# A hybrid attention block: c4 ahead of q's chunk, four staging buffers, V turned at the end of the head, branch products ahead of the weighted sum

## The chip, the cores and the metric

The kernel runs on one core of one Trainium2 chip. The core has five engines with instruction streams of their own: TensorE (PE, with its weight loads listed as PEld), VectorE (DVE), ScalarE (ACT), GpSimd (POOL) and SyncE (SP). They meet through semaphores; an engine carries out its own stream strictly in order, so an instruction that waits also holds up whatever stands behind it. The metric is the device time of one execution in microseconds, and lower is better.

## The reference, cut to what matters

One layer over 512 tokens of width 1024, with 16 learned meta tokens in front (528 in all). All of it is fp32.

```python
xn = rmsnorm(h)
sb_q, sb_k, sb_v, df_q, df_k, df_v = split(xn @ w_in)      # 8 heads of 128 in each branch
# branch A, stick-breaking: z = q.k / sqrt(128), strictly causal
u = where(causal, log_sigmoid(-z), 0); rest = reverse_cumsum(u) - u
o_sb = where(causal, exp(log_sigmoid(z) + rest), 0) @ v
# branch B, differential: two softmax maps of 64 channels each, with bias and chunk mask
o_df = rmsnorm_per_head((softmax(s0) - lam * softmax(s1)) @ v)
merged = sigmoid(gate0) * (o_sb @ w_br_sb) + sigmoid(gate1) * (o_df @ w_br_df)
h = h + merged @ w_out
h = h + (silu(hn @ w_ffn_gate) * (hn @ w_ffn_up)) @ w_ffn_down   # hn = rmsnorm(h)
return rmsnorm(h)
```

## The kernel before

**Numbers in two pieces.** Every fp32 factor of a large product is held as a high piece (a cast, made by ACT) and a low piece (the rest, made by DVE); one product is three matmuls, hi x hi, lo x hi and hi x lo, at lines 227, 228 and 229. A weight chunk is split into `wh` at line 75 (ACT) and `wl` at line 76 (DVE).

**The order of the work.** After an opening (to about 40 us), eight stick-breaking heads run one after another, then eight differential heads, then gates and merge, the output projection, the feed-forward layer and its down projection. A head's attention is a generator (`sb_head`, `df_head`). While it runs, the projections of the next head and pieces of the branch product of an earlier pair of heads are interleaved as "units": each `yield n` of the generator lets n units through, and what is left over runs at the head's end. A scheduler then places the instructions of each engine in a fixed order by its own estimates, near the order in which the program issues them.

**Seven products.** From head `SEVEN` on, k and v of a head are projected together with seven half-size products in place of eight. The units `u1` to `u4` need sums of weight blocks: `c1` splits v's chunk g; `c2` forms the sum s out of k's chunk u, which is staged as `wsu`, and g (lines 173 and 174, on DVE), and splits it; `c3` adds g and u inside `wsu` (line 181) and splits that; `c4` adds into g's second half (line 188) and splits the half. q's chunk is split plainly (`generic`). The list `prep` gives the order in which chunks are prepared: here, for each such head, c1, c2, c3, then q's chunk, then c4, and a chunk of the branch product's weights behind them. A unit that needs an entry first has the list prepared up to `READY` entries further.

**Staging.** SP's queue brings chunks from DRAM in the order of the list `stream`, 512 KB each, into `wst` (three buffers here) or, for a k chunk of such a head, into `wsu` (one buffer in the attention's pool, so that the next k chunk's transfer can only be issued once the split of c3, `wl<-wsu`, has read this one).

**A head's end.** The units `t1` and `t2` (`turn_first`, `turn_rest`) turn the attention weights (lines 493, 507, 510), with the pieces a_h and a_l at lines 495 and 496. `av` (`weighted`) is the weighted sum over V. In a stick-breaking head its result is taken out of a bank of the score tile (two such tiles of two banks, in turn) at lines 590 (o_h) and 591 (o_l); the next head's scores use the same tiles, zA for the first three query blocks and zB for the fourth. `turn` turns V of the next head (vT to vh, vl, vf; lines 469 to 477); here it is one of the units, between the first and the second unit of the branch product. A unit of the branch product (`y_units`) forms two blocks of 128 x 512, copies each out on ACT, and has POOL's queue store it (the first two products of a branch) or add it into DRAM, 256 KB a block; a head carries four blocks.

In a differential head the scores go through `biased` (line 636, two maps of each query block), `maps` makes the softmax, and the evacuations of q (lines 604 and 605) and k (611 and 612) hold copies for both maps; two DMAs of POOL's queue bring halves of dk to the other partitions (line 615).

## Time and profile before

| what | value |
|---|---|
| three runs | 1001.55, 998.5, 1000.55 us; median 1000.55 |
| profiled execution | 998.36 us, its span 996.6 us |
| granted TensorE clock | 0.995 |
| PE / DVE / ACT / POOL busy | 96% / 71% / 60% / 16% |
| stick-breaking heads with seven products (from 108 us) | 28.00 us each, PE busy throughout |
| differential heads (from 248 us) | 31 to 32 us each, PE busy 27.53 to 29.73 us |
| 517 to 632 us (gates, merge, output projection) | PE busy 114.99 of 115 us |
| 665 to 980 us (feed-forward) | PE busy 314.56 of 315 us |

The tensor engine is the busy one; where it is busy throughout, work on the other engines costs nothing unless it makes PE wait. In a timeline the columns are start, duration, engine, line, operation, out<-in, and in brackets the engine's idle time before the instruction with what ended it. `wl<-wsu` and the like name the tiles without buffer numbers.

### The profile page before, as it was taken

To read this page: it belongs to the slowest core of one execution; us is meant where nothing else is said; L and a number is where in the kernel's file an instruction comes from. 1 tells how busy PE (TensorE), PEld (TensorE's weight loads), DVE (VectorE), ACT (ScalarE), POOL (GpSimd) and SP (SyncE) were. 2 spreads that over 40 slices of the span, in tenths; PEclk is the share of its full clock that TensorE was granted. 3 is DMA by queue.
4 is the path that set the end of the run, shared out by engine and by line. 5 is a ranking of instruction groups with operands and counts; after the bars stand their busy time and mean duration, and the time that the engine had idled before them with its cause. 6 is when DMAs were issued, how large, how long until landed. Compare 5 with 4: busy or idle time off the path is not lost.

```text
span 996.6 us, 16149 instructions
## 1 busy us (share of the span) xinstructions
PE 958.2 (96%) x6117; PEld 857.3 (86%) x6117; DVE 711.1 (71%) x1284; ACT 600.8 (60%) x1147; POOL 160.5 (16%) x216
## 2 busy tenths in 40 slices
PE   7999999999989999999999999989999999999996
PEld 4998888889877898778878888879999999988885
DVE  8898687777767977788642633799888888754544
ACT  5666666667577877778772533675555555743533
POOL 4010111111232222323313520000000000000103
PEclk9999999999999999999999999999999999999999
DMA  7212434445654444547838732223333333333212
GB/s 214 86 43 65 127 113 105 109 105 127 148 100 115 97 137 129 105 108 207 174 91 199 228 117 86 84 84 107 103 110 100 113 95 118 102 110 100 92 43 85
DMA packets 140240, 114.12 MB, mean 115 GB/s; under 512 B 4961, under 2 KB 115714, under 8 KB 140162
## 3 DMA queue, kind: packets, MB, share of 16 engines
q1 hardware_dynamic: 129810, 89.29, 29.7%
q0 software_dynamic: 10192, 23.73, 12.4%
q8 instruction: 48, 0.79, 0.3%
q14 instruction: 30, 0.25, 0.1%
q10 hardware_dynamic: 160, 0.07, 0.0%
HBM read 89.87 MB, written 18.87 MB: 109 GB/s over the span
## 4 chain that ended last, share of the span: by engine, by line
PE 66%; DVE 17%; ACT 7%; DMA 5%; issue 4%; POOL 0%; SPq 0%; ACTq 0%; DVEq 0%; POOLq 0%
PE mm L227 15%; PE mm L229 15%; PE mm L228 15%; PE z L227 6%; PE z L229 6%; PE z L228 6%; DMA wsu<-in_w_in_dram 4%; DVE wl L76 3%; DVE pr L636 2%; ACT wh L75 1%; ACT pr L660 1%; DVE dq L605 1%; PE z L493 1%; DVE dk L612 1%; DVE s L578 1%
## 5 line engine op out<-in xcount | busy, mean ns | idle before, releaser
L76 DVE TENSOR_TENSOR wl<-wst,wh 128x1024 fp32r<-128x1024 f32 (+1 forms) x150 | 166.4, 1114 | 90.5 <-ACT wh L75 90.5
L75 ACT CAST wh<-wst 128x1024 fp32r<-128x1024 f32 (+1 forms) x150 | 142.1, 948 | 87.9 <-PE z L229 37.8
L227 PE MATMUL mm<-xT_h,wh 128*128 128x512 f32 (+2 forms) x496 | 168.7, 340 | 0.1
L228 PE MATMUL mm<-xT_l,wh 128*128 128x512 f32 (+2 forms) x496 | 168.4, 340 | 0.4 <-DVE xT_l L828 0.2
L229 PE MATMUL mm<-xT_h,wl 128*128 128x512 f32 (+2 forms) x496 | 167.4, 338 | 0.0
L227 PEld LDWEIGHTS mm<-xT_h,wh 128*128 128x128 f32 x496 | 93.9, 189 | 10.3 <-ACT xT_h L827 1.0
L228 PEld LDWEIGHTS mm<-xT_l,wh 128*128 128x128 f32 x496 | 93.6, 189 | 10.2 <-DVE xT_l L828 0.6
L229 PEld LDWEIGHTS mm<-xT_h,wl 128*128 128x128 f32 x496 | 93.6, 189 | 9.8
L228 PE MATMUL mm<-hT_l,wh 128*128 128x256 f32 x284 | 80.6, 284 | 0.7 <-DVE hT_l L1074 0.7
L227 PE MATMUL mm<-hT_h,wh 128*128 128x256 f32 x284 | 80.5, 285 | 0.6 <-DVE sg L1169 0.6
L229 PE MATMUL mm<-hT_h,wl 128*128 128x256 f32 x284 | 80.2, 283 | 0.0
L227 PE MATMUL mm<-o_h,wh 128*128 128x512 f32 x128 | 53.5, 420 | 9.2 <-DVE dq L605 8.8
L228 PEld LDWEIGHTS mm<-hT_l,wh 128*128 128x128 f32 x284 | 53.8, 189 | 1.1 <-DVE hT_l L1074 1.1
L227 PEld LDWEIGHTS mm<-hT_h,wh 128*128 128x128 f32 x284 | 53.5, 189 | 1.0 <-DVE sg L1169 0.8
L173 DVE TENSOR_TENSOR s<-wsu 128x512 f32<-128x512 f32 x35 | 27.4, 783 | 37.2 <-DMA wsu<-in_w_in_dram 28.4
L229 PEld LDWEIGHTS mm<-hT_h,wl 128*128 128x128 f32 x284 | 53.7, 189 | 0.0
L229 PE MATMUL mm<-o_h,wl 128*128 128x512 f32 x128 | 50.6, 397 | 0.0
L228 PE MATMUL mm<-o_l,wh 128*128 128x512 f32 x128 | 50.3, 394 | 0.0
L76 DVE TENSOR_TENSOR wl<-wsu,wh 128x1024 fp32r<-128x1024 f32 x35 | 42.8, 1223 | 8.9 <-ACT wh L75 8.7
L227 PE MATMUL mm<-t_h,wh 128*128 128x256 f32 x168 | 47.5, 283 | 1.3 <-ACT wh L75 1.0
L475 POOL COPY v_s<-vT 128x16 f32<-128x16 f32 x64 | 22.3, 497 | 163.8 <-DVE vT L405 78.1
L228 PE MATMUL mm<-t_l,wh 128*128 128x256 f32 x168 | 47.2, 281 | 1.1 <-DVE t_l L1089 1.1
(316 smaller groups left out, 2776.4 us busy)
## 6 DMA issues: line engine op xcount, KB each, us to landing
wst<-in_w_in_dram SPq DMA_DIRECT2D x32, 512.0 KB, 4.4
wst<-in_w_ffn_gate_dram SPq DMA_DIRECT2D x22, 512.0 KB, 3.9
wst<-in_w_ffn_down_dram SPq DMA_DIRECT2D x22, 512.0 KB, 3.6
wsu<-in_w_ffn_up_dram SPq DMA_DIRECT2D x21, 512.0 KB, 3.7
wst<-in_w_gate_dram SPq DMA_DIRECT2D x16, 512.0 KB, 4.6
wsu<-in_w_in_dram SPq DMA_DIRECT2D x14, 512.0 KB, 6.5
y_df<-ys POOLq DMA_DIRECT2D x20, 256.0 KB, 5.9
dk<-dk POOLq DMA_DIRECT2D x16, 264.0 KB, 3.6
```

The source lines that it names most:

```text
L75: (hi_copy or nc.scalar.copy)(hi, src)
L76: (lo_eng or nc.vector).tensor_tensor(lo, src, hi.bitcast(F32), op=ALU.subtract)
L173: nc.vector.tensor_tensor(s[:, K2], u[:, K1], u[:, K2], op=ALU.add)
L227: nc.tensor.matmul(ps, lhsT=ah, rhs=bh, start=(start and i == 0), stop=False, skip_group_check=skip)
L228: nc.tensor.matmul(ps, lhsT=ah, rhs=bl, start=False, stop=False, skip_group_check=skip)
L229: nc.tensor.matmul(ps, lhsT=al, rhs=bh, start=False, stop=(stop and i == n - 1), skip_group_check=skip)
L475: nc.gpsimd.tensor_copy(v_s[:, 32 * t:32 * t + NM], vT[:, (t + 1) * P:(t + 1) * P + NM])
L493: nc.tensor.transpose(pt[:, (t - j) * P:(t - j + 1) * P], blocks(t, j * P, (j + 1) * P), ident)
L578: nc.vector.tensor_tensor_scan(f, f, f, 0.0, op0=ALU.add, op1=ALU.bypass)
L605: nc.vector.scalar_tensor_tensor(q[c][b], ps[a], DF_SCALE, q[c][a].bitcast(F32), op0=ALU.mult, op1=ALU.subtract)
L612: nc.vector.scalar_tensor_tensor(k[c][a, 1, s], ps[a], scale, k[c][a, 0, s].bitcast(F32), op0=ALU.mult, op1=ALU.subtract)
L636: nc.vector.tensor_tensor_reduce(po, zz, bb, scale=1.0, scalar=-3.0e38, op0=ALU.add, op1=ALU.max, accum_out=mx[:, t, c:c + 1])
```

## The change

It does four things. Four buffers, not three, for the staged chunks. In `prep`, c4 stands directly behind c3, ahead of the same head's q chunk. `turn` is no longer a unit: it runs at the end of the loop's body, behind the weighted sum and all units, and so vf, vh and vl have one buffer each. And the yields let more units through ahead of the weighted sum. To make room, `y_back` uses the tags of o_h and o_l, and the feed-forward's `sq` has a tag of its own with one buffer.

```diff
--- before.py
+++ after.py
@@ -138,7 +138,7 @@
         elif sevens(key) and key[2] == 1:
             st = fpools["a"].tile([P, KT, P], F32, tag="wsu", name="wsu")
         else:
-            st = wpool.tile([P, k1 - k0, cw], F32, tag="wst", bufs=3, name="wst")
+            st = wpool.tile([P, k1 - k0, cw], F32, tag="wst", bufs=4, name="wst")
         staged.append(st)
         for a, b in ((0, 4), (4, 8)) if n < 2 else ((0, k1 - k0),):
             nc.sync.dma_start(st[:, a:b], view[:, k0 + a:k0 + b, c0:c0 + cw])
@@ -195,7 +195,7 @@
         key = stream[n][0]
         fns = [] if sevens(key) else [generic]
         if sevens(key) and key[2] < 2:
-            fns = [c1, c2, c3] if key[2] else [generic, c4]
+            fns = [c1, c2, c3, c4] if key[2] else [generic]
         for fn in fns:
             prep_at[key if fn is generic else (fn, key[0:2])] = len(prep)
             prep.append((fn, n if fn is generic else key[0:2]))
@@ -461,9 +461,9 @@
 
         def turn():
 
-            vf = ap_.tile([P, 2, P], F32, tag="vf", bufs=2, name="vf")
-            vh = ap_.tile([P, 3, P], F32R, tag="vh", bufs=2, name="vh")
-            vl = ap_.tile([P, 3, P], F32R, tag="vl", bufs=2, name="vl")
+            vf = ap_.tile([P, 2, P], F32, tag="vf", name="vf")
+            vh = ap_.tile([P, 3, P], F32R, tag="vh", name="vh")
+            vl = ap_.tile([P, 3, P], F32R, tag="vl", name="vl")
             pt, p5 = tr_tile(), tr_tile()
             for j in range(4):
                 nc.tensor.transpose(pt[:, j * P:(j + 1) * P], vT[:, j * P:(j + 1) * P], ident)
@@ -585,7 +585,7 @@
         t1()
         yield 1
         t2()
-        yield 1
+        yield 2
         ps = av()
         nc.scalar.copy(o_h, ps)
         nc.vector.tensor_tensor(o_l, ps, o_h.bitcast(F32), op=ALU.subtract)
@@ -679,9 +679,8 @@
         t1, t2, av = attn_out(lambda t, k0, k1: prs[t][:, 0, k0:k1], d, 64)
         yield 3 if h < NH - 1 else 2
         t1()
-        yield 1
         t2()
-        yield 1
+        yield 2
         ps = av()
         of = ap_.tile([P, SEQ], F32, tag="of", name="of")
         sq = ap_.tile([P, SEQ], F32, tag="sq", name="sq")
@@ -941,7 +940,7 @@
                 sg0 = [gate_tile(br) for br in range(2)]
                 units = more + gate(0, 0, sg0[0], AF.Identity) + gate(1, 0, sg0[1], AF.Identity)
             else:
-                units = units + more[0:1] + [turn] + more[1:]
+                units = units + more
             if (br, h) == (0, 0):
                 for i, u in enumerate(sums):
                     units[i] = lambda a=units[i], b=u: (a(), b())
@@ -950,6 +949,8 @@
                     units.pop(0)()
             for u in units:
                 u()
+            if turn:
+                turn()
             d = nd
             if h % 2:
                 todo += [y_units(name, h - 1 + i, o) for i in range(2)]
@@ -973,8 +974,8 @@
 
     def y_back(f):
         got = []
-        for name in ("y_sb", "y_df"):
-            y = mgp.tile([P, SEQ], F32, tag=name, name=name, bufs=2)
+        for name, tag in (("y_sb", "o_h"), ("y_df", "o_l")):
+            y = opool.tile([P, 2, SEQ], F32, tag=tag, name=name)[:, 0]
             nc.sync.dma_start(y, y_part[name][f])
             got.append(y)
         return got
@@ -1029,7 +1030,7 @@
                     step(k, t, c0, c1)
                 cs = slice(half * 512 + c0, half * 512 + c1)
                 nc.vector.tensor_tensor(hres[:, t, cs], hres[:, t, cs], (acc[t] if c0 == 0 else extra)[:, c0:c1], op=ALU.add)
-                sq = pool.tile([P, 512], F32, tag="y_sb", bufs=2, name="sq")
+                sq = pool.tile([P, 512], F32, tag="sq", bufs=1, name="sq")
                 s0, s1 = ssq[t][:, 0:1], ssq[t][:, 1:2]
                 nc.scalar.activation(sq[:, c0:c1], hres[:, t, cs], AF.Square, accum_out=(s1 if half else s0))
                 if half == 0:
```

The same instructions are issued; they stand in another order. On DVE, in a stick-breaking head, between the split of c3 and the next head's scores, before (s_2005 and s_2316 are the sums of two heads; L591 is o_l, L472 V's low piece):

```order
L76 TENSOR_TENSOR wl<-wsu,wh 128x1024
L514 COPY a_s<-z 16x32 x2
L188 TENSOR_TENSOR wst<-s_2005,wst 128x512
L591 TENSOR_TENSOR o_l<-z,o_h 128x512
L472 TENSOR_TENSOR vl<-tr,vh 128x384
L173 TENSOR_TENSOR s_2316<-wsu 128x512
L76 TENSOR_TENSOR wl<-wst,wh 128x1024
```

and with the change:

```order
L76 TENSOR_TENSOR wl<-wsu,wh 128x1024
L514 COPY a_s<-z 16x32 x2
L188 TENSOR_TENSOR wst<-s_2005,wst 128x512
L76 TENSOR_TENSOR wl<-wst,wh 128x512
L173 TENSOR_TENSOR s_2316<-wsu 128x512
L174 TENSOR_TENSOR s_2316<-s_2316,wst 128x512
L591 TENSOR_TENSOR o_l<-z,o_h 128x512
L472 TENSOR_TENSOR vl<-tr,vh 128x384
```

c4's split (128x512) has moved up ahead of the next head's sum, and the two halves of that sum, L173 and L174, have moved ahead of o_l and V's piece.

Further on in the same head on DVE, around the scans (L578; the split `wl<-wst,wh 128x1024` is q's chunk), before:

```order
L173 TENSOR_TENSOR s_2316<-wsu 128x512
L76 TENSOR_TENSOR wl<-wst,wh 128x1024
L384 TENSOR_TENSOR vT<-mm,qq 128x264
L574 SCALAR_TENSOR_TENSOR s<-z,e 128x832
L574 SCALAR_TENSOR_TENSOR s<-z,e 128x528
L578 SCALAR_TENSOR_TENSOR s<-s 128x144
L578 SCALAR_TENSOR_TENSOR s<-s 128x272
L578 SCALAR_TENSOR_TENSOR s<-s 128x416
L578 SCALAR_TENSOR_TENSOR s<-s 128x528
L579 TENSOR_TENSOR s<-z,s 128x832
L579 TENSOR_TENSOR s<-z,s 128x528
L396 SCALAR_TENSOR_TENSOR qq<-mm,qq 128x264
```

and with the change:

```order
L574 SCALAR_TENSOR_TENSOR s<-z,e 128x832
L384 TENSOR_TENSOR vT<-mm,qq 128x264
L578 SCALAR_TENSOR_TENSOR s<-s 128x144
L578 SCALAR_TENSOR_TENSOR s<-s 128x272
L578 SCALAR_TENSOR_TENSOR s<-s 128x416
L574 SCALAR_TENSOR_TENSOR s<-z,e 128x528
L579 TENSOR_TENSOR s<-z,s 128x832
L578 SCALAR_TENSOR_TENSOR s<-s 128x528
L76 TENSOR_TENSOR wl<-wst,wh 128x1024
L396 SCALAR_TENSOR_TENSOR qq<-mm,qq 128x264
L579 TENSOR_TENSOR s<-z,s 128x528
```

q's split stood second, ahead of the whole chain; now it stands behind the last scan.

On DVE in a differential head, between the split of c3 and the first biased scores (L636), before (L496 is a_l, L514 the small transposed blocks):

```order
L76 TENSOR_TENSOR wl<-wsu,wh 128x1024
L496 TENSOR_TENSOR a_l<-z,a_h 128x384
L496 TENSOR_TENSOR a_l<-z,a_h 128x256
L472 TENSOR_TENSOR vl<-tr,vh 128x384
L188 TENSOR_TENSOR wst<-s_4775,wst 128x512
L514 COPY a_s<-z 16x64 x2
L173 TENSOR_TENSOR s_5145<-wsu 128x512
L636 ISA pr,mx<-z,bias 128x144
```

and with the change:

```order
L76 TENSOR_TENSOR wl<-wsu,wh 128x1024
L496 TENSOR_TENSOR a_l<-z,a_h 128x384
L514 COPY a_s<-z 16x64 x2
L188 TENSOR_TENSOR wst<-s_4790,wst 128x512
L76 TENSOR_TENSOR wl<-wst,wh 128x512
L173 TENSOR_TENSOR s_5160<-wsu 128x512
L174 TENSOR_TENSOR s_5160<-s_5160,wst 128x512
L472 TENSOR_TENSOR vl<-tr,vh 128x384
L636 ISA pr,mx<-z,bias 128x144
```

L173 stood ahead of L636 already; L174, V's piece and c4's split now stand there too, and V's piece behind L173.

## The prediction

> **What bounds the kernel now.** I read the page first, then the busy times by stretch of one head each, the waits, and the timelines of one head of each branch.
>
> ```profile
> PE 958.2 (96%) x6117; PEld 857.3 (86%) x6117; DVE 711.1 (71%) x1284; ACT 600.8 (60%) x1147; POOL 160.5 (16%) x216
> PE 66%; DVE 17%; ACT 7%; DMA 5%; issue 4%; POOL 0%; SPq 0%; ACTq 0%; DVEq 0%; POOLq 0%
> L173 DVE TENSOR_TENSOR s<-wsu 128x512 f32<-128x512 f32 x35 | 27.4, 783 | 37.2 <-DMA wsu<-in_w_in_dram 28.4
> ...
> 164.00:192.00 28.00, 28.00 (x185) 24.99 (x183) 20.55 (x33) 18.59 (x34) 5.04 (x8) 1.00 0.52 113
> 279.00:310.00 31.00, 27.53 (x177) 24.51 (x176) 24.64 (x61) 22.88 (x54) 9.62 (x13) 1.00 0.54 119
> 342.00:373.00 31.00, 28.72 (x184) 25.54 (x183) 24.16 (x61) 22.85 (x54) 8.13 (x13) 1.00 0.41 119
> 517.00:632.00 115.00, 114.99 (x510) 95.13 (x511) 47.15 (x58) 43.42 (x67) 33.90 (x24) 1.00 0.54 151
> ```
>
> In the stretches the columns are the length, then PE, PEld, DVE, ACT, POOL. A stick-breaking head is all PE (28.00 of 28): nothing can be gained there, and each new PE wait is paid in full. A differential head leaves PE idle 2.3 to 3.5 us of 31: that is all there is to gain. Gates, merge and output projection (517 to 632) are full; y's new staging tags and sq's single buffer change nothing on PE there, so I cost them at 0; in the opening, one c2 sum moves up, also 0 (at worst one such sum, 0.8). All the rest is the two kinds of head.
>
> The idle time of the differential heads has two owners:
>
> ```profile
> PE mm L227 <- DVE dq L605: 8.8, 6, 2.5
> PE z L227 <- DVE a_l L496: 6.1, 6, 1.0
> ```
>
> Columns: total us, times, longest. Six heads, so 1.5 and 1.0 us a head: a projection product waits for the bank that q's evacuation frees, and the weighted sum waits for DVE's piece of the weights.
>
> **The change in the stick-breaking heads.** With c4 ahead of q's chunk, DVE meets L173, which waits for the staged chunk wsu, ahead of the evacuation o_l (L591), and o_l holds a score bank that the next head's last scores need. Before, o_l stood ahead:
>
> ```profile
> 166.62 1.22 DVE L76 TENSOR_TENSOR wl<-wsu,wh 128x1024 fp32r<-128x1024 f32 x1
> 168.73 0.69 DVE L188 TENSOR_TENSOR wst<-s,wst 128x512 f32<-128x512 f32 x1
> 170.81 0.69 DVE L591 TENSOR_TENSOR o_l<-z,o_h 128x512 fp32r<-128x512 f32 x1 [1.39 <-ACT o_h L590]
> 171.42 0.55 DVE L472 TENSOR_TENSOR vl<-tr,vh 128x384 fp32r<-128x384 f32 x1
> 173.13 0.69 DVE L173 TENSOR_TENSOR s<-wsu 128x512 f32<-128x512 f32 x1 [1.17 <-DMA wsu<-in_w_in_dram]
> ...
> 167.92 0.37 SPq L144 DMA_DIRECT2D wsu<-in_w_in_dram  x1
> ...
> 163.95 0.86 PE L493 MATMUL z<-ident,s 128*128 128x128 f32 x5
> 174.86 0.37 PE L227 MATMUL z<-kh,qh 128*128 128x264 f32 x1
> ```
>
> The single wsu buffer is still released by `wl<-wsu` alone. Count from E = 163.95, the end of u4. PE does the same matmuls between u4 and those scores (B = 174.86), so it arrives at E + 10.9 as before. Two more a_l pieces stand ahead of `wl<-wsu` than before; I put its end at E + 4.65 (it was E + 3.9, 0.75 less) and the DMA 0.06 behind. With D from issue to L173's start, o_l ends at E + 4.7 + D + 0.62 (L173) + 0.62 (L174) + 0.69 (o_l): the scores wait S = D - 4.2 (rounded, with 0.06 for the signal). V's turn, vl, stands behind o_l and costs nothing there. What was D?
>
> ```profile
> 140.41 0.38 SPq L144 DMA_DIRECT2D wsu<-in_w_in_dram  x1
> 144.50 0.69 DVE L173 TENSOR_TENSOR s<-wsu 128x512 f32<-128x512 f32 x1 [0.38 <-DMA wsu<-in_w_in_dram]
> ...
> GB/s 0 0 0 0 0 155 93 0 0 0 185 124 185 201 216 170 216 247 147 205 309 325 352 348 305 301 301 294 301 282 340 309 259 247 243 216 216 185 185 201
> DMA packets 1298, 1.02 MB, mean 192 GB/s; under 512 B 34, under 2 KB 1058, under 8 KB 1298
> q0 software_dynamic: 258, 0.49, 61.5%
> ...
> 348.20 0.37 SPq L144 DMA_DIRECT2D wsu<-in_w_in_dram  x1
> ...
> DMA packets 1309, 1.37 MB, mean 188 GB/s; under 512 B 80, under 2 KB 1104, under 8 KB 1309
> q0 software_dynamic: 269, 0.85, 48.9%
> ...
> DMA to landing us min/median/max: 4.1/6.5/7.1
> ```
>
> 4.1 us in the first two heads concerned (140.41 to 144.50), whose branch products are only stored; 5.2 in the next three (167.92 to 173.13), where they are added to memory. The two windows of the DMA view run from issue to L173: 1.02 MB in the head at 167.92, 0.49 of it branch products from POOL's queue, and 1.37 MB in 7.2 us in the differential head at 348.20. Both ran near 190 GB/s, so another 0.26 MB costs about 1.3 us at the mean, 0.9 at the 300 GB/s that the faster of the 40 slices reach.
>
> ```profile
> 173.05 0.86 POOL L729 DMA_DIRECT2D y_sb<-sg  x1 [3.00 <-ACT sg L725]
> ```
>
> The third product's DMA went out 5.1 us after wsu's. Now all four are formed before the weighted sum, and I put the third at 2 and the fourth at 3 us after wsu's: one more 256 KB in the window. I take D = 6.1 in three heads (S = 1.9) and 4.6 in two (S = 0.4): **+6.5 us**. Bounds: D as before gives 0.9 x 3 = 2.7; D = 7.2, as in the differential heads, gives 3.0 x 3, with 1.0 x 2 for the two: 11.
>
> The Trainium skill, page "DMA: Bandwidth & Descriptors", section "Issuing engines are not separate DMA queues", says that DMAs of all issuing engines run on the same 16 DMA engines and interleave. By it the products of POOL's queue lengthen SP's wsu, and the term is the 6.5; were the queues independent it would be the 2.7. The 4.1 against 5.2 above speaks for the rule.
>
> The second new wait is q's own chunk, now split behind c4. Before, its wl was formed at once after L173; now it stands behind the scan of the second score pair:
>
> ```profile
> 174.38 1.23 DVE L76 TENSOR_TENSOR wl<-wst,wh 128x1024 fp32r<-128x1024 f32 x1 [0.55 <-ACT wh L75]
> 179.00 0.43 DVE L384 TENSOR_TENSOR vT<-mm,qq 128x264 f32<-128x264 f32 x1 [3.40 <-ACT e L573]
> 179.35 1.63 DVE L574 SCALAR_TENSOR_TENSOR s<-z,e 128x832 f32<-128x832 f32 x2
> 180.90 3.13 DVE L578 TENSOR_TENSOR_SCAN s<-s 128x144 f32<-128x144 f32 x4
> 183.94 1.61 DVE L579 TENSOR_TENSOR s<-z,s 128x832 f32<-128x832 f32 x2
> 183.55 0.40 PE L229 MATMUL mm<-xT_h,wl 128*128 128x512 f32 x1
> ```
>
> From L384 (B + 4.1) DVE has 0.35 for it, about 1.9 for three scans, 0.6 and 0.9 for one L574 and one L579, 1.2 for the last scan and 1.2 for wl: B + 10.2. PE's first matmul on q's wl was at 183.55, B + 8.7, and has five small matmuls (0.4) moved ahead of it: 1.1 to 1.2 us of wait in each of five heads, **+6 us**. Bounds 0.3 to 1.9 a head (the second if the first L574 too falls behind L384, 0.8): 1.5 to 9.5.
>
> **The change in the differential heads.** All four products now stand between u4 and the weighted sum, so they cover q's evacuation and the a_l pieces: both waits above go. What is late next is the same L173, ahead of the biased scores (L636):
>
> ```profile
> 339.01 0.28 PE L227 MATMUL mm<-tB,wh 128*128 128x264 f32 x1
> 346.91 1.23 DVE L76 TENSOR_TENSOR wl<-wsu,wh 128x1024 fp32r<-128x1024 f32 x1
> 355.43 0.93 DVE L173 TENSOR_TENSOR s<-wsu 128x512 f32<-128x512 f32 x1 [4.38 <-DMA wsu<-in_w_in_dram]
> 356.38 0.31 DVE L636 CUSTOM_DVE_ANT_0 pr<-z,bias 128x144 f32<-128x144 f32 x1
> 356.61 0.30 DVE L636 CUSTOM_DVE_ANT_0 pr<-z,bias 128x144 f32<-128x144 f32 x1
> 358.96 0.34 PE L632 MATMUL z<-dk,dq 128*128 128x400 f32 x1
> 370.49 0.28 PE L227 MATMUL mm<-tB,wh 128*128 128x264 f32 x1
> ```
>
> The head repeats every 31.48 us (339.01 to 370.49). The third scores (358.96) need both L636: done at 356.92, so they had 2 us in hand. From there to the next start of u4's block at 370.49 are 11.53 us with no wait. In the new order DVE has 0.45 us less ahead of `wl<-wsu` (one split fewer, one a_l piece more, counted against the exponentials of the last map): its end falls 8.7 after that start, where it was 9.1. Then 0.06, D', 0.62 for L173, 0.62 for L174, 0.47 for vl, 0.54 for L636, 11.53: the period is 22.55 + D', or PE's own 28.5 where that is more. L174 and vl, new ahead of L636, are 1.1 us of it. D' was 7.2 here (348.20 to 355.43) and near the median landing of 6.5 elsewhere, with two products bunched at wsu's issue. Now the third and fourth fall in its window too, while one dk copy has left it: 0.23 MB more, 0.8 to 1.2 us. I take D' = 7.7, period 30.25, gain 1.2 us in each of six heads: **-7.3 us**. Bounds: PE's 28.5 (-17.5) and D' = 9 (+0.5, no gain).
>
> **Sum** against the profiled 998.36: +6.5 + 6 - 7.3 = +5.2, 1003.6; the median of the runs, 1000.55, lies 2.2 above that execution, so I write 1004. From 0.3% (3 us) on, a measurement of this kernel tells a change.
>
> **Rivals.** (1) The DMAs do not slow wsu, and q's split finds room: 0.9 x 3 in place of 6.5, 0.5 x 5 in place of 6, and D' = 6.8 (29.35, 2.1 x 6 = -12.7): -7.5, **991**, faster. For it: products queued behind POOL's issue may start late. Against it: 4.1 against 5.2. It decides where D stays under about 5.2. (2) Contention the other way: D = 7.2, D' = 9: 11 + 6 + 0.5, **1016**. For it: four products of 256 KB now meet one wsu. Against: 300 GB/s in the fast slices. (3) The change does not do what it says: gain and loss cancel, as with D = 5.6 (4.2), q's wait 0.6 (3) and -7.2: 0, **998 to 1000**.
>
> **Chances.** Forecast 0.46, (1) 0.28, (2) 0.12, (3) 0.14. Faster is (1) and little else, 0.29; slower is (2) and 0.40 of the forecast, 0.52; same is (3) and the forecast's near edge, 0.19. The forecast's own range is 999 to 1010; with (1) and most of (2), 990 to 1015.
>
> **What would show it.** In a stick-breaking head the wait `z L227 <- DVE o_l L591` of 1 to 2 us and a wait of `mm L229` for `wl L76` of about 1 us, the head over 30 us; in a differential head no wait for dq or a_l, but one of `z L632` for L636, the head near 30.3; wsu's median landing above 6.5. No o_l wait means (1); 3 us of it means (2). The forecast is wrong if the stick-breaking heads stay at 28 us.

## The result, and the profile after

The changed kernel takes 1027.67 us (median of four runs, 1022.83 to 1028.4), the kernel before 1000.92 in the same session: 1.0262 times as long, 95% interval 1.0225 to 1.0298. It is slower by 26.7 us. The forecast was 1004 us, 3.5 above the median of 1000.55 (its sum alone was +5.2), and the far end of the range, 1015, was 14 above it.

The profiled execution took 1026.95 us, span 1025.2. From its page, the busy times, the shares of the chain of waits, and L173's group (columns: count | busy, mean ns | idle time before it, and what ended it):

```profile
PE 969.8 (95%) x6117; PEld 859.3 (84%) x6117; DVE 713.2 (70%) x1284; ACT 598.3 (58%) x1147; POOL 158.1 (15%) x216
PE 54%; DVE 22%; DMA 9%; ACT 9%; issue 5%; POOL 0%; SPq 0%; DVEq 0%; ACTq 0%; POOLq 0%
L173 DVE TENSOR_TENSOR s<-wsu 128x512 f32<-128x512 f32 x35 | 26.3, 752 | 40.6 <-DMA wsu<-in_w_in_dram 32.4
```

PE's part of the chain fell from 66% to 54%, while the transfers' part rose from 5 to 9% and DVE's from 17 to 22%. The longest waits of PE, after (total us, times, longest):

```profile
PE z L227 <- DVE o_l L591: 8.6, 4, 3.2
PE z L632 <- DVE mx L636: 6.9, 5, 1.9
PE mm L227 <- ACT qq L389: 4.4, 5, 0.9
PE z L493 <- ACT s L580: 3.0, 5, 1.1
PE mm L229 <- DVE wl L76: 2.7, 6, 0.6
PE mm L227 <- DVE dq L605: 2.2, 5, 1.5
```

The first and the fifth had been named in the prediction. dq fell from 8.8 to 2.2 and a_l's 6.1 are gone, also as forecast. The second was named, but not priced as a loss; the third, 4.4 us for ACT's evacuation L389, was not foreseen.

Of the other signs, the heads of over 30 us came in four of the five stick-breaking heads. wsu's median landing did not rise above 6.5 us as was forecast; it is 6.3. So the 0.8 to 1.2 us of added contention that the prediction priced into the differential heads are not seen: D' is 6.99 us in the mean of five heads, where it was 6.82 before.

**Where the time is.** PE starts each head's products on `tB` at a fixed place of the head's projections, so these starts cut the run into comparable parts. From PE's timeline, before, then after:

```profile
97.80 0.28 PE L227 MATMUL mm<-tB,wh 128*128 128x264 f32 x1
...
237.52 0.28 PE L227 MATMUL mm<-tB,wh 128*128 128x264 f32 x1
...
457.53 0.28 PE L227 MATMUL mm<-tB,wh 128*128 128x264 f32 x1
```

```profile
100.40 0.28 PE L227 MATMUL mm<-tB,wh 128*128 128x264 f32 x1
...
257.25 0.28 PE L227 MATMUL mm<-tB,wh 128*128 128x264 f32 x1
...
483.82 0.28 PE L227 MATMUL mm<-tB,wh 128*128 128x264 f32 x1
```

| part, us | before | after | difference |
|---|---|---|---|
| opening and first heads, to the first mark | 97.80 | 100.40 | +2.6 |
| five stick-breaking heads, first to second mark | 139.72 | 156.85 | +17.1 |
| change of branch and six differential heads, second to third mark | 220.01 | 226.57 | +6.6 |
| from there to the end of the span | 539.07 | 541.4 | +2.3 |

Forecast for the second row was +12.5 and for the third -7.3; the first and the last stood at 0.

The third part has seven periods, the change of branch first. Before they are 29.36, 33.27, 31.48, 31.47, 31.46, 31.50 and 31.47; after, 29.26, 33.47, 33.63, 32.97, 32.98, 33.64 and 30.62. Four heads in the middle lose 7.3 us together. The last head gains 0.85, and it is the only one without an L173, since it has no next head to prepare. It serves as a control inside the same kernel.

**A stick-breaking head after** (SP's, DVE's and PE's timelines, start and duration first):

```profile
177.16 0.37 SPq L144 DMA_DIRECT2D wsu<-in_w_in_dram  x1
...
183.62 0.69 DVE L173 TENSOR_TENSOR s<-wsu 128x512 f32<-128x512 f32 x1 [3.04 <-DMA wsu<-in_w_in_dram]
184.34 0.69 DVE L174 TENSOR_TENSOR s<-s,wst 128x512 f32<-128x512 f32 x1
185.06 0.69 DVE L591 TENSOR_TENSOR o_l<-z,o_h 128x512 fp32r<-128x512 f32 x1
...
185.81 0.39 PE L227 MATMUL z<-kh,qh 128*128 128x264 f32 x1 [2.25 <-DVE o_l L591]
197.72 0.50 PE L229 MATMUL mm<-xT_h,wl 128*128 128x512 f32 x1 [0.56 <-DVE wl L76]
```

D, from wsu's issue to L173, is 6.46 us here. DVE stands 3.04 us in front of L173, then forms both sums, then o_l, and PE waits 2.25 for it. The chain is the one that the prediction drew. The wait for wl at 197.72 is the one that it named for q's late split.

**A differential head after** (DVE, PE, ACT):

```profile
335.94 1.22 DVE L76 TENSOR_TENSOR wl<-wsu,wh 128x1024 fp32r<-128x1024 f32 x1
...
345.29 0.69 DVE L173 TENSOR_TENSOR s<-wsu 128x512 f32<-128x512 f32 x1 [4.66 <-DMA wsu<-in_w_in_dram]
...
347.44 0.30 DVE L636 CUSTOM_DVE_ANT_0 pr<-z,bias 128x144 f32<-128x144 f32 x1
...
347.89 0.42 PE L632 MATMUL z<-dk,dq 128*128 128x400 f32 x1 [1.36 <-DVE mx L636]
...
352.26 1.03 ACT L75 CAST wh<-wst 128x1024 fp32r<-128x1024 f32 x1
353.19 0.37 ACT L389 COPY qq<-mm 128x264 f32<-128x264 f32 x1
...
353.61 0.39 PE L227 MATMUL mm<-tB,wh 128*128 128x264 f32 x1 [0.89 <-ACT qq L389]
```

Before, the second L636 ended 2 us ahead of the third scores; now it ends at 347.74 and the third scores start right behind it. The exponentials that need the bias pass are later on ACT, and the evacuation L389 stands behind them and makes PE wait once more. From the bias pass's maximum to the end of L389 ACT needs 5.33 us here and 5.37 before, so L389 is late because the bias pass is. That holds although a whole weight cast now stands ahead of it (1.03 us, where half a one, 0.60, stood).

### The profile page after: what moved, and what is told of

Same layout as the page of the kernel before. It is cut to its first block, busy times and chain, and to the rows that moved or that the text cites. A ratio compares the mean times of both kernels' runs of the same rounds, so it can differ in the third digit from the quotient of the medians.

```text
span 1025.2 us, 16143 instructions
## 1 busy us (share of the span) xinstructions
PE 969.8 (95%) x6117; PEld 859.3 (84%) x6117; DVE 713.2 (70%) x1284; ACT 598.3 (58%) x1147; POOL 158.1 (15%) x216
## 4 chain that ended last, share of the span: by engine, by line
PE 54%; DVE 22%; DMA 9%; ACT 9%; issue 5%; POOL 0%; SPq 0%; DVEq 0%; ACTq 0%; POOLq 0%
PE mm L227 12%; PE mm L229 12%; PE mm L228 12%; DMA wsu<-in_w_in_dram 7%; PE z L227 5%; PE z L229 5%; PE z L228 5%; DVE wl L76 4%; DVE s L578 2%; ACT pr L660 2%; DVE pr L636 2%; ACT wh L75 2%; DVE s L173 1%; DVE dk L612 1%; DVE pr L666 1%
## 5 line engine op out<-in xcount | busy, mean ns | idle before, releaser
L173 DVE TENSOR_TENSOR s<-wsu 128x512 f32<-128x512 f32 x35 | 26.3, 752 | 40.6 <-DMA wsu<-in_w_in_dram 32.4
L75 ACT CAST wh<-s 128x1024 fp32r<-128x1024 f32 x35 | 36.7, 1048 | 29.6 <-PE z L228 15.8
L475 POOL COPY v_s<-vT 128x16 f32<-128x16 f32 x64 | 17.4, 318 | 219.8 <-DVE vT L384 90.7
```

What stands on the lines that cost most here:

```text
L75: (hi_copy or nc.scalar.copy)(hi, src)
L173: nc.vector.tensor_tensor(s[:, K2], u[:, K1], u[:, K2], op=ALU.add)
L475: nc.gpsimd.tensor_copy(v_s[:, 32 * t:32 * t + NM], vT[:, (t + 1) * P:(t + 1) * P + NM])
```

## The experiments

The kernel before lay between 999.17 and 999.87 us (medians) in these sessions. "W" in the expectations is the theory of the prediction: L173, held by wsu, in front of what PE needs.

### Each part of the change alone

**Only c4's place**, added to the kernel before:

```diff
-            fns = [c1, c2, c3] if key[2] else [generic, c4]
+            fns = [c1, c2, c3, c4] if key[2] else [generic]
```

> The kernel before with one part alone: c4's sum stands ahead of q's chunk; three staging buffers, V's turn and the yields stay as before. In this order DVE keeps o_l ahead of L173, and q's split stands behind both scans and both L579. Theory W (the loss is DVE's wait for wsu standing ahead of o_l and of the biased scores): no wait of the scores for o_l in the stick-breaking heads, time 1001 to 1007, the rest being q's late split. Theory Q (the loss is q's split and what it delays): about 1.5 us in each of five stick-breaking heads and about as much in the differential heads, 1010 to 1018. My prediction's own reading, that c4's place is what puts L173 ahead of o_l, would give the o_l wait here too, 1015 to 1020.

1045.49 us, ratio 1.0454 (1.0420 to 1.0487): the worst kernel of the study, and none of the expectations. o_l stays ahead of L173. DVE's waits:

```profile
DVE s L174 <- DMA wst<-in_w_in_dram: 32.4, 8, 7.1
```

DVE waits up to 7.1 us for v's staged chunk in front of L174, ahead of the scans, and PE for the scans' results. That c4 ahead of q's chunk holds, with three buffers, one that v's next chunk needs is a reading of the order that no run here separates. What is shown is that c4's move alone brings this wait, and not the one for o_l; the prediction was wrong to make c4's place by itself the owner of L173's place.

**Only four buffers** (three to four for `wst`, one for vf, vh and vl, the merge's tags), in the kernel before:

```diff
-            st = wpool.tile([P, k1 - k0, cw], F32, tag="wst", bufs=3, name="wst")
+            st = wpool.tile([P, k1 - k0, cw], F32, tag="wst", bufs=4, name="wst")
...
-            vf = ap_.tile([P, 2, P], F32, tag="vf", bufs=2, name="vf")
+            vf = ap_.tile([P, 2, P], F32, tag="vf", name="vf")
```

> The kernel before with four buffers for the staged chunks and nothing else (one buffer each for vf, vh, vl and the new tags, so that it fits). v's chunk comes a head earlier; the order on DVE now has L174 and L181 right behind L173, ahead of the scans and of the biased scores; o_l stays ahead of L173. Theory W: in the stick-breaking heads DVE is idle there until the scans, so nothing; in the differential heads L174 and L181 use 1.3 of the 2.0 us in hand, so nothing; 998 to 1004. Theory B (four buffers alone move enough on DVE to cost what all changed kernels with four of them lost in the first heads, 4.5 us, and some in the rest): 1004 to 1012.

1010.65 us, 1.0117 (1.0098 to 1.0135). The stick-breaking heads stay at 27.9 us but for the first (28.39); the differential ones rise from 31.5 to between 32.7 and 34.2, and the last, which has no L173, takes 30.0.

**Only V's turn at the end**, in the kernel before:

```diff
-                units = units + more[0:1] + [turn] + more[1:]
+                units = units + more
...
+            if turn:
+                turn()
```

> The kernel before with V's turn alone moved to the head's end (two buffers each stay). o_l stays ahead of L173, q's split ahead of the scans, and c4's split moves behind the last scan. Theory W: nothing in the stick-breaking heads, nothing or a little in the differential heads, 998 to 1003. Theory T (undoing the turn gave 12 us, so the turn itself is the cost: its transposes and its piece on DVE in the way of the next scores): 1005 to 1012.

1012.09 us, 1.0129 (1.0091 to 1.0168). Again the stick-breaking heads are untouched (27.9 to 28.3) and the differential ones take 33.1 to 37.4.

**Only the yields**, in the kernel before:

```diff
-        yield 1
+        yield 2
...
-        yield 1
         t2()
-        yield 1
+        yield 2
```

> The kernel before with the new yields alone, so the products stand ahead of the weighted sum. On DVE o_l stays ahead of L173, q's split ahead of the scans, and in the differential heads only L173 stands ahead of the biased scores. Theory W: the stick-breaking heads stay at 28 us; the differential heads lose the waits for dq and a_l (2.4 us a head) and are bounded by L173 and the biased scores or by PE's 28: 29.5 to 30.5 a head, 988 to 995. Theory C (products ahead of the weighted sum leave no cover behind it): 1 to 2 us a head for o_l and the transposes, 1003 to 1012.

997.37 us, 0.9977 (0.9964 to 0.9990): the only part that gains, and less than W had it. The differential heads take 31.0 to 31.3 us from the third on. The prediction said that all four products ahead of the weighted sum would cover dq and a_l; with the yields alone PE still waits 6.9 us for dq in all and 2.9 for a_l.

So no single part costs the stick-breaking heads what the whole does, except c4's with three buffers, and by another wait.

### The change with one part undone

**V's turn a unit again** (the diff of the turn reversed):

> The changed kernel with V's turn put back as a unit between the two units of the branch product (one buffer each for vf, vh, vl as in the change). In this order DVE has o_l ahead of L173 in three of the five stick-breaking heads; in two L173 stands ahead of o_l. In the differential heads L173 and L174 stay ahead of the biased scores. Theory W: the o_l waits and the slow clock behind them go in the three heads that lost most (7 to 9 us of the 11), the differential heads stay: 1017 to 1021. Theory Q: nothing but V's place changes, 1025 to 1028. Theory C (products all ahead of the weighted sum leave no cover behind it): the turn as a unit moves cover behind the weighted sum again, all o_l waits go in all five heads, 1012 to 1016.

1015.44 us, 1.0163 (1.0148 to 1.0179): below W's range and inside that of theory C (1012 to 1016). The waits for o_l are gone: o_l stands ahead of L173 in four of five heads, by the scheduler's choice, and in the first, where L173 is ahead, the changed kernel had no wait either. The differential heads take 32 to 33.7, the last 30.4. This run does not tell C, the missing cover behind the weighted sum, from L173's place; the one with L173 behind o_l, further down, speaks against C.

**The yields undone**:

> The changed kernel with the yields put back as before (one unit after each of the two turns, in both branches). DVE has o_l ahead of L173 in four of five stick-breaking heads; L173 and L174 stay ahead of the biased scores in the differential heads, where products stand behind the weighted sum again. Theory W: the o_l waits go (9 us and 1.7 of slow clock); in the differential heads the old waits for dq and a_l (2.4 us a head) come back and the wait for the biased scores shrinks, 1013 to 1018. Theory Q: 1023 to 1028, since q's split and the scans keep their order. Theory C: as W in the stick-breaking heads, and the differential heads fall back to 31.5 us, 1008 to 1012.

1024.56 us, 1.0265 (1.0243 to 1.0286), not W's figure but inside theory Q's range (1023 to 1028). The o_l waits go (o_l stands ahead of L173 in four of five heads), and the same order of time comes back elsewhere:

```profile
PE mm L227 <- ACT qq L383: 8.4, 8, 2.6
PE z L632 <- DVE mx L636: 8.3, 6, 2.0
PE z L493 <- ACT s L580: 4.7, 6, 1.2
```

The trace leads from the first of them back to L173, by another road than Q's. From the third stick-breaking head on DVE waits 3.7 to 4.3 us in front of L173, V's piece vl stands behind it, ACT waits for vl, and ACT's evacuation L383, which PE needs, stands behind that:

```profile
181.57 0.69 DVE L173 TENSOR_TENSOR s<-wsu 128x512 f32<-128x512 f32 x1 [3.69 <-DMA wsu<-in_w_in_dram]
183.51 0.55 DVE L472 TENSOR_TENSOR vl<-tr,vh 128x384 fp32r<-128x384 f32 x1
184.09 0.27 ACT L473 COPY vf<-tr 128x128 f32<-128x128 f32 x1 [3.27 <-DVE vl L472]
186.82 0.39 ACT L383 COPY qq<-mm 128x264 f32<-128x264 f32 x1
187.26 0.39 PE L227 MATMUL mm<-tA,wh 128*128 128x264 f32 x1 [1.96 <-ACT qq L383]
```

**c4 behind q's chunk again**, the rest of the change kept:

> The changed kernel with c4 back behind q's chunk; four buffers, V's turn and the yields as changed. DVE has L173 ahead of o_l in all five stick-breaking heads, but L174 behind it, and q's split ahead of the scans. Theory W (DVE's wait for a chunk that stands ahead of o_l, the scans or the biased scores is the loss, whichever part of the change puts it there): the o_l wait stays, 0.6 us less a head (6 us and a slow clock at times), q's waits of about 1 us a head go, the differential heads lose as before the undoing: 1016 to 1021. Theory P (c4's place is the loss, as my prediction had it): 1000 to 1006.

1014.3 us, 1.0155 (1.0117 to 1.0194), below W's range. Three of the stick-breaking heads are back at 27.96 us (the first two take 28.43 and 28.26) although L173 still stands ahead of o_l: D is 5.2 to 5.4, DVE waits at most 0.5 us in front of it, L174 stands behind o_l, and q's split is early again. The differential heads stay at 30.4 to 35.2 us.

**Two wsu buffers, three for wst**, in the changed kernel, so that L173 need not wait:

```diff
-            st = fpools["a"].tile([P, KT, P], F32, tag="wsu", name="wsu")
+            st = fpools["a"].tile([P, KT, P], F32, tag="wsu", bufs=2, name="wsu")
...
-            st = wpool.tile([P, k1 - k0, cw], F32, tag="wst", bufs=4, name="wst")
+            st = wpool.tile([P, k1 - k0, cw], F32, tag="wst", bufs=3, name="wst")
```

> The changed kernel with two buffers for wsu and three for the other staged chunks: the next k chunk is fetched a head earlier, so nothing has to wait for it, while products, turn and c4 stay as changed. Theory W: no wait of DVE for the transfer, no wait of the scores for o_l (9 us and 1.7 of slow clock gone) and none for the biased scores in the differential heads (1.5 us in each of seven), 1002 to 1009. Theory Q: the scans and q's split stay late, 1020 to 1028. Theory C: PE still waits for o_l right behind the weighted sum, 1 to 2 us a head, 1012 to 1018.

1030.1 us, 1.0302 (1.0279 to 1.0325). L173 no longer waits and the o_l waits are gone, but L174, right behind it, waits for v's chunk (DVE, then PE):

```profile
DVE s L174 <- DMA wst<-in_w_in_dram: 43.2, 11, 5.7
...
PE mm L227 <- ACT qq L389: 14.9, 6, 4.3
PE z L493 <- ACT s L580: 13.3, 8, 3.7
```

A buffer taken from one chunk and given to the other moves the wait by one instruction. In all of these variants more than one thing moves, since the scheduler re-sorts DVE for each of them; the cause is not isolated by any.

### L173's place

So the next edits add an order for L173 and nothing else. The scheduler sorts the rows anew even so, and what else moved is said with each. **L173 behind o_l** in the stick-breaking heads of the changed kernel, by an order on DVE without a wait:

```diff
-        nc.vector.tensor_tensor(s[:, K2], u[:, K1], u[:, K2], op=ALU.add)
+        first = nc.vector.tensor_tensor(s[:, K2], u[:, K1], u[:, K2], op=ALU.add)
+        if behind:
+            tc.add_manual_dep(first.ins, behind[-1].ins.name, mybir.DependencyInfo(
+                mybir.DependencyClass.NoSync, mybir.DependencyReason.DATA), reason="behind")
...
-        nc.vector.tensor_tensor(o_l, ps, o_h.bitcast(F32), op=ALU.subtract)
+        behind.append(nc.vector.tensor_tensor(o_l, ps, o_h.bitcast(F32), op=ALU.subtract))
```

> The changed kernel with one order more on DVE: in the stick-breaking heads L173 is formed only behind the head's o_l (L591); the differential heads are as changed. Theory W (it is L173, held by the chunk, ahead of o_l that costs the stick-breaking heads their time): the waits of z L227 for o_l (8.6 us in the changed kernel) and the 1.7 us of slow clock go, L173 runs unwaited or waits with nothing behind it, the heads come back to 29 to 30 us (q's split behind the scans stays, about 1 us each): 1015 to 1019. Theory Q (the score banks are late for other reasons, the late q split and the exps behind it above all): the o_l wait goes but the heads stay over 31 us, 1023 to 1028. Both expect the differential heads at about 33 us.

1012.82 us (the profiled execution 1017.3), 1.0134 (1.0117 to 1.0151), two below W's range and far from Q's. PE's marks (the lines of this kernel are four further down):

```profile
246.89 0.28 PE L231 MATMUL mm<-tB,wh 128*128 128x264 f32 x1
...
475.87 0.28 PE L231 MATMUL mm<-tB,wh 128*128 128x264 f32 x1
```

The first mark is at 100.27, so the five heads take 146.62 us, 10.2 less than in the changed kernel: the 8.6 of o_l and 1.7 more (below). The products still stand ahead of the weighted sum here and V's turn behind it, so theory C's cover is missing as before, and the o_l waits are gone. The differential heads take 228.98, no less than the 226.57; one of them has a 2.51 us wait for dk and a slow clock, which the median run can lack.

Beside L173, some 240 of PE's 6117 instructions, 60 of DVE's 1284 and 40 of ACT's stand elsewhere than in the changed kernel, all of them in the stick-breaking heads and the change of branch. L173's share of the 10.2 isn't separated from theirs.

**L173 also behind the bias pass** in the differential heads:

```diff
-            nc.vector.tensor_tensor_reduce(po, zz, bb, scale=1.0, scalar=-3.0e38, op0=ALU.add, op1=ALU.max,
-                                           accum_out=mx[:, t, c:c + 1])
+            ins = nc.vector.tensor_tensor_reduce(po, zz, bb, scale=1.0, scalar=-3.0e38, op0=ALU.add, op1=ALU.max,
+                                                 accum_out=mx[:, t, c:c + 1])
+            if (t, c) == (1, 1):
+                behind.append(ins)
```

so that L173 follows the biased scores of the second query block, which the third scores wait for.

> The kernel of sum_behind_ol, and in the differential heads L173 is formed only behind the biased scores (L636) of the first of the last pair. Theory W (in these heads, too, it is L173's wait that delays the bias pass and with it the third scores): the waits of z L632 and the mx L636 waits of 1.1 to 2 us a head go, period 33 to 30 to 31 us, 1.5 to 2.5 us in each of six heads, so 9 to 15 under sum_behind_ol: 1002 to 1009. Theory Q (the exponentials and q's evacuation on ACT and DVE, bunched differently by the yields, are what is late): the mx wait goes, qq L389 or pr L666 waits grow in its place, period over 32: 1013 to 1019.

1001.92 us (ten runs), 1.0029 (1.0018 to 1.0041): W, at the low edge of its range.

```profile
246.33 0.28 PE L231 MATMUL mm<-tB,wh 128*128 128x264 f32 x1
...
459.62 0.28 PE L231 MATMUL mm<-tB,wh 128*128 128x264 f32 x1
```

213.29 us for the differential heads: 13.3 less than in the changed kernel, 6.7 less than before. Three of the periods are 29.96 or 29.97 us, one is 30.37, the last 29.29, and no wait for mx or for L389 is left; one is 34.18, with a wait of 2.42 us for a transfer of dk and a slow clock behind it. Against the kernel above, the rows of PE, POOL and SP are the same, and some 55 instructions of DVE and 35 of ACT moved, in the differential heads, among them a weight cast that now stands ahead of exponentials.

What remains in the stick-breaking heads is a period of 29.24 to 29.28 us (29.65 in the first) in place of 27.94. The wait that the trace names there is 1.09 us of PE for ACT's weights (L584 in this kernel, L580 in the changed one), not one for q's wl. The next kernel shows that c4's place owns it; by which road isn't shown.

**And c4 behind q's chunk** on top of it:

```diff
-            fns = [c1, c2, c3, c4] if key[2] else [generic]
+            fns = [c1, c2, c3] if key[2] else [generic, c4]
```

> The kernel of sum_behind_both with c4 behind q's chunk again, as before the change; the four buffers, the turn behind the weighted sum, the new yields and L173's place stay. Theory W (all that is left of the loss is q's split behind the scans): the stick-breaking heads go from 29.2 to 27.9 to 28.1 us and the differential ones stay at 30.0 to 30.4, so 8 to 10 us under sum_behind_both: 991 to 995. Theory B (the four buffers, one each of V's parts, cost by themselves in heads 0 to 2 and in the differential heads, as in the runs that had them without L173's new place): 1000 to 1006, differential heads over 31.

995.12 us, 0.9944 (0.9922 to 0.9967): W's upper edge, and faster than before. The stick-breaking heads are at 27.96. The differential ones take 30.5 to 32.0, where W had up to 30.4; PE still waits 6.3 us in all for `pr` (L672 in this kernel, L666 in the changed one), so the order with c4 behind q's chunk is not free there. The profiled execution took 1000.4, the longest of the four, and some 300 of PE's instructions and 100 of DVE's stand elsewhere than in the kernel above.

**The yields alone, with L173 behind o_l and the bias pass**, in the kernel before (the two diffs above):

> The kernel before with the changed yields (all four branch products ahead of the weighted sum) alone, and L173 behind o_l in the stick-breaking heads and behind the biased scores in the differential ones. With the new yields alone it was 997.4 of 999.7. Theory W (L173 in front of the bias pass costs the differential heads part of their 2.3 to 3.5 us of PE idle time): their period falls from 31.2 to 30.0 to 30.6, 990 to 994. Theory Q (the waits for dq and a_l, 0.6 to 2 us a head, are what is left, and L173 is covered by them): 996 to 1000, period 31 or more.

992.87 us, 0.9938 (0.9924 to 0.9953), the fastest of the study, and W's middle. This is the cleanest of these tests: against the kernel with the yields alone the rows of PE, POOL and SP are the same, and 18 instructions of DVE and 6 of ACT moved. L173 no longer waits, and PE's wait for dq falls from 6.9 us to 4.7 in all. The differential heads take 30.25 to 30.5 us from the third on. PE's part of the chain of waits is now:

```profile
PE 80%; DVE 10%; ACT 5%; issue 2%; DMA 2%; POOL 1%; SPq 0%; DVEq 0%; ACTq 0%; POOLq 0%
```

L173's wait costs the kernel with the old buffers, turn and c4's place, too, without a line of PE's waits naming it: in the kernel before L173 stood ahead of the bias pass with 2 us in hand. The order for L173 took the ratio from 0.9977 to 0.9938, which is 3.9 us. Without the yields it was not tried.

### What makes D long

**One staging buffer less** in the list's look-ahead of the changed kernel, to have the next chunk go out later:

```diff
-STAGE, READY, START = 5, 3, 4
+STAGE, READY, START = 4, 3, 4
```

> The changed kernel with one staging buffer for wst fewer (four for five), DVE's order the same. It asks what lengthens D, the time from wsu's issue to L173, from 5.2 to 6.5 to 7.0 us in the stick-breaking heads. Theory S (the next staged chunk, issued 3 us behind wsu): with a buffer fewer that chunk goes out later than 4.5 us behind wsu, D is 5.2 to 5.6, the o_l waits fall from 2 to 3 us to 0.8 to 1.2 each, 1019 to 1023 unless v's or q's chunk itself comes late. Theory P (the bunched branch products): D stays 6.5 to 7.0 wherever the chunk's issue falls, o_l waits 2 to 3 us, 1025 to 1029.

1029.05 us, 1.0305 (1.0289 to 1.0320). It tells nothing of the two theories: the chunk still went out 3.4 us behind wsu (175.77 and 179.22 in one head), and D stayed at 6.6 to 7.5. The rows are the same but for one transfer of SP's.

**Branch products stored, not added**, in the changed kernel:

```diff
-                    nc.gpsimd.dma_start(y_part[name][f], ys, accum_op=ALU.add)
+                    nc.gpsimd.dma_start(y_part[name][f], ys)
```

> The changed kernel, every engine's order the same, but the branch products of the third head on are stored over the partial sums instead of being added to them in memory (so the two branch outputs hold the last pair's products alone). Theory P (the products of POOL's queue, 0.64 MB of them in wsu's window where before had 0.48, make D longer): D falls to 4.4 to 5.2 in the third to fifth stick-breaking heads, where it was 6.5, 7.0 and 5.7, and under 6 in the differential ones; the o_l wait falls from 8.6 to under 4 us, 1010 to 1018. Theory S (the staged chunk issued 3 us behind wsu on the same queue): D stays over 6 in these heads, o_l waits of 7 us or more, 1023 to 1028.

1017.54 us, 1.0173 (1.0152 to 1.0194): P. The order of every engine is the same and the next chunk goes out 3.0 to 3.5 us behind wsu as before, yet D falls from 6.46, 7.02 and 5.67 to 4.32, 5.13 and 4.24 in the last three stick-breaking heads, and the o_l waits from 8.6 to 3.3 us. The DMA view from wsu's issue to L173 in the same head, of the changed kernel and of this one (packets, MB, share of the 16 engines' time):

```profile
q0 software_dynamic: 351, 0.65, 57.9%
q1 hardware_dynamic: 1041, 0.52, 33.0%
```

```profile
q1 hardware_dynamic: 1040, 0.52, 47.1%
q0 software_dynamic: 111, 0.38, 21.4%
```

POOL's queue (q0) took 57.9% of the engines' time in the one and 21.4% in the other; SP's queue (q1) moved 0.52 MB, which is wsu's own 512 KB, so the next chunk had hardly begun. In the kernel before q0 moved 0.47 to 0.49 MB in these three windows (D 4.98 to 5.25). That the products are added and not stored makes D long here: 0.65 MB of additions held the engines for more time than their share of the bytes would have it (57.9% of 6.46 us, against 21.4% of 4.32 us for 0.38 MB). The kernel leaves the sums out, so it is a test and not a candidate. Since every engine does the same in the same order, it is the cleanest evidence for the stick-breaking heads: with a shorter D they take 151.48 us in place of 156.85.

What is not shown is that one more product in the window did it, as the prediction had it. The windows of the changed kernel hold 0.65, 0.64 and 0.49 MB, and in the third D grew with 0.02 MB more; and with the yields alone, which gather the products in the same way, D is only 5.40, 5.54 and 5.62. In the differential heads D is still 5.7 to 6.5 us without the additions, not under 6 throughout, and three of them still take 32.94 or 32.95: L173 takes 1.57 to 1.76 us in them, and with D' makes the same 8.10.

**The square of the head's output on DVE**, not POOL, in the changed kernel:

```diff
-        eng = nc.gpsimd if h < NH - 1 else nc.vector
+        eng = nc.vector
```

> The changed kernel with the square of the differential head's output and its split (sq, sql) formed on DVE in place of POOL in all heads. It asks why L173 took 1.55 to 1.82 us in some differential heads and 0.69 in the others. Theory G (POOL's tensor operation sql running beside it holds DVE up): every L173 of the differential heads takes 0.68 to 0.70 us; the time is within 6 us of the changed kernel's, since DVE now does 2 x 0.7 us more a head. Theory D (DMA writes into SBUF, or the queue, slow it): L173 still takes over 1 us in some of these heads.

1028.05 us, 1.0281 (1.0266 to 1.0296). Every L173 of the heads takes 0.69 us: G. In the changed kernel it took up to 1.82 beside POOL's `sql`:

```profile
377.12 1.82 DVE L173 TENSOR_TENSOR s<-wsu 128x512 f32<-128x512 f32 x1 [2.85 <-DMA wsu<-in_w_in_dram]
```

```profile
377.11 1.30 POOL L76 TENSOR_TENSOR sql<-sq,sqh 128x512 fp32r<-128x512 f32 x1 [0.73 <-ACT sqh L75]
```

The time does not fall; sq and sql now stand in DVE's own row, and PE waits 7.9 us for sql.

## Why the prediction was wrong

**The stick-breaking heads: +12.5 forecast, +17.1 measured. The mechanism of the o_l wait is right and its size small; the size of q's split was met in part by luck.**

- *o_l behind L173: +6.5 forecast, 8.65 measured* (1.73, 2.25, 3.21 and 1.46 in four of five heads). D was put at 6.1 in three heads and 4.6 in two; it was 6.46, 7.02, 5.67 and 4.38, 4.68. That the added products lengthen D is shown by the kernel that stores them; the reason given, one more of them in the window, stays open. In the second head D was 4.68, and the wait still 1.73: there q's second sum L181 (0.68 us) stands ahead of o_l, too, and PE is at the scores 10.4 us behind u4, not 10.9.
- *q's split behind the scans: +6 forecast (1.1 to 1.2 a head), 6.5 measured.* With L173 out of the way the head takes 29.23, 1.29 more than 27.94, and the kernel with c4 behind q's chunk gives it back. But the wait named, PE for wl, is only 0.56 us in three heads and 0.17 in the first; in the second PE waits for ACT's weights (0.64 and 1.12) instead. The rest is longer busy time of PE (28.5 for 27.94), so the sum came out near for reasons that the prediction had not given.
- *Not in the sum at all: 1.7 us of slow clock* behind one o_l wait (last section).

**The differential heads: -7.3 forecast, +6.6 measured. This is the failed step.** It was "the period is 22.55 + D'", with D' = 7.7 and so 30.25; it was 33.0 to 33.6 in the five heads that have an L173. D' itself was put too long (7.7; measured 5.94, 8.07, 6.27, 6.57, 8.09). What failed is the fixed rest. From u4 to u4, four heads take 24.87 us + D' + L173's own time: 33.62 and 33.64 with 8.76 and 8.78 for the two, 32.98 twice with 8.10 and 8.11. The prediction's 22.55 without its 0.62 for L173 is 21.93, so the rest was 2.94 short. Two of its terms make 2.67 of that, 0.27 lies in the smaller ones, and L173's own time was a third error:

- *"11.53 us with no wait" from the third scores to the next u4.* It was 13.24 in each of five heads, 1.7 more. The third scores came 19.7 to 20.4 us behind u4, hardly later than before (19.95); but before, the bias pass ended at 17.9, 2 us ahead of them, and now it ends with them. These 2 us had kept ACT's exponentials ahead of the evacuations of k and q. The prediction followed the late pass to PE and not to ACT; the waits for L383 and L389 (0.18 and 0.89 a head) and PE's restarts behind them are what it missed. The last head, without L173, shows the other case: 11.52 us from the third scores to u4, and a period of 30.62.
- *The end of `wl<-wsu`, put at 8.7 behind u4:* it was 9.66 (9.92 in the first head).
- *L173, put at 0.62:* 0.69 alone, 0.82 in the first head, and up to 1.82 in those where it runs beside POOL's sql. The row that the prediction itself quoted (355.43, 0.93 us) already showed a long one.

With L173 behind the bias pass the part takes 213.29, 6.7 less than before, and the waits for a_l are gone and those for dq 0.2 us in all heads but one. So the gain that the prediction saw in the yields is there once L173 doesn't hold DVE. That 6.7 is near 7.3 is luck: the -7.3 was counted with L173's wait as what bounds the period, and the 213.29 hold a head of 34.18.

**The opening and the tail: 0 forecast, +2.6 and +2.3 measured.** The mark before the first is 1.0 us later (75.02 for 74.03). With only the four buffers it is at 75.26, but with L173 behind both, which has four buffers too, at 74.18; the cause of this 1.0 isn't shown. The head that follows takes 1.6 us longer (25.38 for 23.77); with c4 behind q's chunk it takes 24.1, so there q's late split costs what it does in the five that were counted. In the tail the clock fell once between 690 and 700 us (granted 0.83, before 1.00); that explains 1.7 of the 2.3, the rest is open.

**The rivals.** (1), faster by D as before, fell with D. (2), 1016 by contention, had the right side, but its D' of 9 was not what cost the time. (3), gain and loss cancelling at 998 to 1000, fell because the gain never came; the heads' loss was there. That the kernel would be slower came out right, but of the two parts that made up the forecast only the first had the right sign.

c4's place, which the prediction took as the owner of the new order, owns it only together with the turn and the yields. With the turn or the yields undone o_l stands ahead of L173 in four of five heads, with c4's move alone in all; with c4 undone L173 stays ahead and hardly waits.

## What to carry to other kernels

When an instruction that waits for a transfer moves ahead of others in an engine's row, cost not only what PE needs from behind it but every engine that reads from there: a lead of 2 us that is used up shows first as another engine's late evacuation. Where a scheduler re-sorts a row for every edit, undoing parts of a change tells little. Ask for the one instruction's place by an order of its own, compare every engine's row in the two traces for what else moved with it, and believe the time as far as little did. A head that lacks the instruction, or a kernel with the same rows and a shorter transfer, is a control that needs no such caution. And look for the same instruction in the kernel before: with the yields and L173 behind o_l and the bias pass, it became faster than by the yields alone.

## What the runs showed of the hardware

**The clock fell behind some PE waits and not behind others.** The changed kernel by stretch (length, busy PE, PEld, DVE, ACT, POOL, granted clock, DMA share, GB/s): the 2.25 us wait that ends at 185.81 and what follows, and the stretch behind the 3.21 us wait that ends at 219.8:

```profile
185.90:187.30 1.40, 1.40 (x12) 1.35 (x13) 0.92 (x2) 1.04 (x3) 0.00 (x0) 1.00 0.88 176
187.30:190.10 2.80, 2.80 (x16) 2.80 (x15) 1.02 (x1) 2.20 (x5) 0.00 (x0) 0.51 0.02 6
...
219.90:223.40 3.50, 3.50 (x29) 3.45 (x30) 1.68 (x3) 3.15 (x6) 0.00 (x0) 1.00 0.13 34
```

After 2.25 us the clock was halved about 1.5 us later, for 3.4 us, which costs 1.7; after 3.21 us it was not. In the kernel with L173 behind both, a 2.42 us wait for a dk transfer that ended at 420.45 was followed by it at once (granted 0.50 from 421.10 to 423.90).

The traces show what tells them apart. The slow stretches of the changed kernel start at 23.50, 187.34 and 692.51 us, which are 48 and 148 times 3.413 us apart: they lie on a fixed grid, and what counts is PE's idle time inside one step of it. The step before 187.34 held 1.89 us of idle time. The 3.21 us wait (216.60 to 219.81) was split by the grid at 218.06 into 1.46 and 1.75. A wait of 1.73 us shows it best: in the changed kernel the grid splits it into 0.61 and 1.12, and nothing follows; with the products stored it lies within one step, and the clock is halved behind it:

```profile
151.86:155.28 3.42, 1.69 (x13) 1.30 (x12) 3.10 (x5) 1.11 (x4) 0.00 (x0) 1.00 0.73 226
155.28:158.69 3.41, 3.41 (x18) 3.30 (x17) 1.02 (x1) 2.12 (x5) 0.00 (x0) 0.50 0.00 0
```

Over the traces of this case every step with more than 1.82 us idle was followed by a slow stretch, and none with less than 1.45; between the two both happened.

The Trainium skill, page "TensorE: Matmul & The Clock Gate", section "Part 1: The HAM clock gate (the 'warmup' mystery)", says that the clock is halved after an idle window of about 3.4 us, and that the windows run freely and do not reset when a kernel starts. The length of the slow stretch and the grid agree; but here about half a window of idle time was enough, and the measurement decides.

**DVE's sum took 1.82 us beside POOL's.** L173 started 0.01 us behind sql and ended 0.53 behind its end (POOL's spans are rough, so the end of sql may be off). The Trainium skill, page "SBUF — State Buffer", section "SBUF: two separate sides", says that a DVE operation with two inputs in SBUF and a GpSimd operation that reads SBUF lock each other out for a whole instruction. The trace agrees: 0.69 us alone, and 0.69 in every head once sql was not on POOL.
